# Differential attention's output norm, per tile of 128 tokens inside attention in place of per head behind it

## The chip, the cores and the metric

The kernel runs on one core of a Trainium2 chip. What counts is the device time of one execution in microseconds (us), the median of several runs. A core has five engines with a queue each that runs in order: TensorE (PE, matmuls and transposes), VectorE (DVE), ScalarE (ACT), GpSimd (POOL) and SyncE (SP), which here issues the loads. Matmul results lie in PSUM, eight banks of 512 float32 for each of 128 partitions.

## The reference, cut to what matters

A block with three token mixers, two layers deep (the delta rule "a", gated linear attention "b", differential attention "c"), whose outputs are normed, projected and merged through gates. This is the part on the third:

```python
def attend(qb, k, v):
    p = jax.nn.softmax(jnp.einsum('bhmqd,bhmkd->bhmqk', qb, k), axis=-1)
    return jnp.einsum('bhqk,bhkd->bhqd', p[:, :, 0] - lam_f * p[:, :, 1], v)
...
def out(o):
    o = _rmsnorm(o, gn) * (1.0 - lam_init)
    return o.transpose(0, 2, 1, 3).reshape(o.shape[0], o.shape[2], HC * DVC)
...
def merge(ya, yb, yd, gates):
    ga, gb, gd = jnp.split(jax.nn.sigmoid(gates), 3, axis=-1)
    return (ga * (ya @ w_o_a) + gb * (yb @ w_o_b) + gd * (yd @ w_o_c)) @ w_out
```

There are four heads of 128 output features, and 256 latent and 256 context tokens. In layer 0 all 512 tokens are queries: the first 256 (context) see 256 keys, the others 512. In layer 1 only the 256 latent tokens are queries, with 512 keys. The norm `_rmsnorm` runs over a head's 128 features, so it is independent for each token and head.

## The kernel before

Activations are kept transposed: features on the partitions, tokens along the free axis. The words of `PLAN[l]` are the steps of a layer's mixer in program order; both plans have "... hb dif mb hc ... mc": output norm of b, attention, merge of b, output norm of c, merge of c. A scheduler takes this program, and moves an instruction ahead on its engine as soon as its operands and its buffers are there, so steps that don't depend on each other interleave. Buffers come from rings: a new tile takes the next slot of its ring in program order, and can be written only when the tile that had the slot before is used up.

The rings that bear on the change: `pm`, three PSUM banks, for the chains of the stream of weight matmuls; `pq`, five PSUM banks, for everything else, attention included; `sd`, six SBUF slots with tag "d", for short-lived tiles of 512 columns, among them the square `sq` and the reciprocal root `rs` of a norm and the gates `sg` of a merge; `sm`, eight slots, for the exponentials `e` and transposed probabilities `PT` of attention.

`diff` (attention) runs over tiles of 128 queries, and in a tile over the four heads. A head is two score matmuls (L1052), for each the row maximum (L1053), its negation (L1054) and an exponential with row sums (L1056); then reciprocal, scaling and combination of both on DVE (L1059 to L1062), transposes on PE (L1065), a copy out of PSUM (L1067) and the matmuls with v (L1069, here "PV") into the bank `oc`. When four heads are done, one copy (L1070) puts the tile into `oT`, of 4 x 512 columns in layer 0, 4 x 256 in layer 1.

`head_out` for "c" goes head by head over all tokens: square (L842, ACT), a matmul with a matrix of ones that sums over the partitions (L844), into a bank of `pm`, Ln and Exp for the reciprocal root (L410 and L411, ACT), a multiply by gain and root (L853, DVE), and the split into a high and a low float32r part `yh`, `yl` (L269 ACT, L270 DVE) that the merge's matmuls read.

`merge` goes over four pairs of output chunks. For a pair it computes two gates (unless they were computed earlier and are fetched): a projection of the hidden state, PE's "pm<-hh,whl" (L274 to L276, 24 matmuls a gate), and a sigmoid of Exp, Ln and Exp on ACT (L402 to L404) in a tile `sg`. Then two chains of 12 matmuls with `wo`, "pm<-yh,whl". All stream matmuls come in threes (high by high, high by low, low by high: L274, L275, L276). L350 are the small matmuls of the modulation vectors.

Of the kernel before, what the change touches and what calls it, by code (L numbers as in the profile page):

```python
# [13 lines left out]
AF = mybir.ActivationFunctionType  # L14
OP = mybir.AluOpType
# [183 lines left out]
class Prog:  # L199
# [611 lines left out]
    def gates_ahead(self, l, j, H, count):  # L811
# [5 lines left out]
        for _ in range(count):  # L817
            pr = len(done)
            done.append(pr)
            for c, p in enumerate(self.proj(l, U_G + 3 * pr + j, H, 256 * l)):  # L820
                s = self.sd([512], "sg")[:, :n]
                self.sigmoid(s, p)
                self.nc.scalar.dma_start(g[pr // 2][:, 2 * (pr % 2) + c], s)

    def head_out(self, l, oT, gn, H, u, name):

        nc = self.nc
        c0 = 256 * l
        n = 512 - c0
        zs = self.stashed.get((l, "z" + name))  # L830
        if l == 0:
            yh = self.ch([4, 512], "yh", F32R)
            yl = self.ch([4, 512], "yl", F32R)
        else:
            y = self.ch([2, 4, 256], "yhl", F32R)
            yh, yl = y[:, 0], y[:, 1]
        for h in range(4):
            o = oT[:, h]
            if zs is None and u is not None and h % 2 == 0:
                pz = self.proj(l, u + h // 2, H, c0)  # L840
            sq = self.sd([512], "sq")
            nc.scalar.activation(sq[:, :n], o, AF.Square)  # L842
            ps = self.pm()
            nc.tensor.matmul(ps[:, :n], self.ones, sq[:, :n], start=True, stop=True)  # L844
            if zs is not None:
                rs = self.rstd(ps[:, :n], n, 1.0 / 128)
                if h == 0:
                    z = self.fetch(zs)
                nc.vector.tensor_mul(o, o, rs[:, :n])
                nc.vector.tensor_mul(o, o, z[:, h])  # L850
            elif u is None:
                rs = self.rstd(ps[:, :n], n, 1.0 / 128)
                nc.vector.scalar_tensor_tensor(o, o, gn, rs[:, :n], op0=OP.mult, op1=OP.mult)  # L853
            else:

                pv = next(pz)
                z = self.sd([512], "z")
                nc.scalar.activation(z[:, :n], pv, AF.Exp, scale=-1.0)
                nc.vector.scalar_tensor_tensor(o, o, gn, pv, op0=OP.mult, op1=OP.mult)
                nc.scalar.activation(z[:, :n], z[:, :n], AF.Ln, bias=self.one)  # L860
                nc.scalar.activation(sq[:, :n], ps[:, :n], AF.Ln, bias=self.eps, scale=1.0 / 128)
                nc.vector.scalar_tensor_tensor(z[:, :n], sq[:, :n], 0.5, z[:, :n], op0=OP.mult, op1=OP.add)
                nc.scalar.activation(z[:, :n], z[:, :n], AF.Exp, scale=-1.0)
                nc.vector.tensor_mul(o, o, z[:, :n])
            self.split(yh[:, h], yl[:, h], o)
        if self.dbg is not None and f"{name}{l}" in self.dbg:
            nc.sync.dma_start(self.dbg[f"{name}{l}"][:, :, c0:512], oT)
        return yh, yl
# [170 lines left out]
    def diff(self, l, q, k, vC):  # L1039
        nc = self.nc  # L1040
        mm = nc.tensor.matmul
        oT = self.ch([4, 512 - 256 * l], "oTc")
        for qt in range(2 * l, 4):
            nk = 256 if qt < 2 else 512
            cs = slice((qt - 2 * l) * 128, (qt - 2 * l + 1) * 128)
            o = self.pq((4, 128), "oc")
            for h in range(4):
                E, r = [], self.ti([4], "r")
                for m in range(2):
                    ms = slice(64 * m, 64 * m + 64)  # L1050
                    p = self.pq()
                    mm(p[:, :nk], q[ms, h, cs], k[ms, h, :nk], start=True, stop=True)  # L1052
                    nc.vector.tensor_reduce(r[:, m:m + 1], p[:, :nk], axis=AX.X, op=OP.max)  # L1053
                    nc.vector.tensor_scalar(r[:, m:m + 1], r[:, m:m + 1], -1.0, None, op0=OP.mult)  # L1054
                    e = self.sm([512], "e")
                    nc.scalar.activation(e[:, :nk], p[:, :nk], AF.Exp, bias=r[:, m:m + 1],  # L1056
                                         accum_out=r[:, 2 + m:3 + m])
                    E.append(e[:, :nk])
                nc.vector.reciprocal(r[:, 2:4], r[:, 2:4])  # L1059
                nc.vector.tensor_mul(r[:, 3:4], r[:, 3:4], self.nlam[l])  # L1060
                nc.vector.tensor_scalar(E[0], E[0], r[:, 2:3], None, op0=OP.mult)
                nc.vector.scalar_tensor_tensor(E[0], E[1], r[:, 3:4], E[0], op0=OP.mult, op1=OP.add)  # L1062
                tp = self.pq((4, 128), "tp")
                for j in range(nk // 128):
                    nc.tensor.transpose(tp[:, j], E[0][:, j * 128:(j + 1) * 128], self.C("ident"))  # L1065
                PT = self.sm([4, 128], "PT")
                nc.scalar.copy(PT[:, :nk // 128], tp[:, :nk // 128])  # L1067
                for j in range(nk // 128):
                    mm(o[:, h], vC[:, j, h * 128:(h + 1) * 128], PT[:, j], start=j == 0, stop=j == nk // 128 - 1)  # L1069
            nc.scalar.copy(oT[:, :, cs], o)  # L1070
        return oT


# [499 lines left out]
```

## Time and profile before

| | us |
|---|---|
| median of three runs | 2596.59 |
| lowest and highest of them | 2590.91, 2604.6 |
| the profiled execution's own time | 2588.37 |
| its span, first to last instruction | 2586.3 |
| PE busy in the span | 2444.9 (95%) |
| DVE busy | 1716.4 (66%) |
| ACT busy | 1416.6 (55%) |
| mean granted clock of PE, 1.00 being 2.4 GHz | 0.973 |

The times of instructions come from the profiled execution, so a sum of them is to be held against its 2588.37. The granted clock is 1.00 or 0.50 at any moment (2.4 or 1.2 GHz); values between are means over a stretch. Attention ("dif") of layer 0 lies at about 600 to 704 us of the span, that of layer 1 at about 1600 to 1686.

### The profile page before, as it was taken

The numbers are of one execution on the slowest core, as the hardware profiler recorded it, in microseconds if no ns is written. First come the engines' busy times: TensorE is split into PE (matmuls) and PEld (weight loads), VectorE is DVE, ScalarE is ACT, GpSimd is POOL, SyncE is SP. The second block draws the span as 40 slices with busy tenths as digits, with TensorE's granted clock in tenths as the row PEclk, the third lists the DMA queues.
The fourth block names the chain that finished last, engine by engine and source line by source line (L and its number), as shares of the span: only waits on it lengthen the run. The fifth ranks groups of instructions, "written<-read, shape, count | busy, mean of one in ns | idle before, by whom it ended". The sixth has DMA issues, their size and how long they took to land.

```text
span 2586.3 us, 35865 instructions
## 1 busy us (share of the span) xinstructions
PE 2444.9 (95%) x13712; PEld 1965.9 (76%) x13712; DVE 1716.4 (66%) x3130; ACT 1416.6 (55%) x2352; POOL 88.2 (3%) x216
## 2 busy tenths in 40 slices
PE   6998999999998999998978999998999999999997
PEld 4786776676676888886867878797878878878876
DVE  5585447756545434336684475767989888988987
ACT  4764343235553332335853433666877777777775
POOL 0000001100120000000000010010000000000000
PEclk8999899999998999999988999998999999999999
DMA  6344332122131223222362232257979899899994
GB/s 266 129 160 157 107 139 99 49 74 74 67 137 66 100 82 120 93 79 85 112 225 77 68 113 81 104 188 288 377 273 355 341 342 356 344 350 353 341 367 182
DMA packets 72707, 473.13 MB, mean 183 GB/s; under 512 B 8208, under 2 KB 10384, under 8 KB 19664
## 3 DMA queue, kind: packets, MB, share of 16 engines
q1 hardware_dynamic: 68208, 464.73, 48.3%
q10 hardware_dynamic: 4320, 6.03, 0.6%
q8 instruction: 110, 1.80, 0.3%
q14 instruction: 69, 0.57, 0.1%
HBM read 463.65 MB, written 7.08 MB: 182 GB/s over the span
## 4 chain that ended last, share of the span: by engine, by line
PE 70%; DVE 6%; ACT 3%; DMA 2%; issue 1%; POOL 0%; ACTq 0%; DVEq 0%; POOLq 0%
PE pm L275 16%; PE pm L274 16%; PE pm L276 16%; PE y L276 3%; PE y L275 3%; PE y L274 3%; PE la L985 1%; DMA raw<-in_win_dram 1%; PE pq L1052 1%; DVE whl L270 1%; PE pm L350 1%; PE tp L1352 1%; PE ob L996 1%; PE ob L998 1%; DVE zq L973 1%
## 5 line engine op out<-in xcount | busy, mean ns | idle before, releaser
L270 DVE TENSOR_TENSOR whl<-raw,whl 128x512 fp32r<-128x512 f32 (+2 forms) x490 | 330.7, 681 | 330.0 <-ACT whl L269 326.7
L274 PE MATMUL pm<-hh,whl 128*128 128x512 f32 (+2 forms) x1264 | 475.6, 378 | 21.3 <-ACT whl L269 7.8
L269 ACT CAST whl<-raw 128x512 fp32r<-128x512 f32 (+2 forms) x490 | 289.6, 600 | 357.1 <-PE pm L276 273.5
L276 PE MATMUL pm<-hh,whl 128*128 128x512 f32 (+2 forms) x1264 | 467.7, 371 | 7.4 <-DVE whl L270 7.4
L275 PE MATMUL pm<-hl,whl 128*128 128x512 f32 (+2 forms) x1264 | 468.3, 371 | 0.0
L270 DVE TENSOR_TENSOR wp<-rawc,wp 128x1024 fp32r<-128x1024 f32 x261 | 313.7, 1222 | 36.6 <-ACT wp L269 30.5
L274 PEld LDWEIGHTS pm<-hh,whl 128*128 128x128 f32 (+1 forms) x1264 | 243.0, 192 | 70.8 <-ACT whl L269 9.2
L269 ACT CAST wp<-rawc 128x1024 fp32r<-128x1024 f32 x261 | 268.1, 1051 | 21.0 <-PE y L276 11.4
L276 PEld LDWEIGHTS pm<-hh,whl 128*128 128x128 f32 (+1 forms) x1264 | 242.3, 192 | 48.9 <-DVE whl L270 8.4
L275 PEld LDWEIGHTS pm<-hl,whl 128*128 128x128 f32 (+1 forms) x1264 | 243.0, 192 | 43.2 <-issue 7.1
L270 DVE TENSOR_TENSOR wlo<-raw,whi 128x1024 fp32r<-128x1024 f32 x176 | 210.0, 1222 | 34.1 <-ACT whi L269 31.7
L275 PE MATMUL pm<-wlo,hg 128*128 128x512 f32 x530 | 212.1, 400 | 1.6 <-DVE wlo L270 1.4
L274 PE MATMUL pm<-whi,hg 128*128 128x512 f32 x530 | 211.2, 399 | 0.0
L276 PE MATMUL pm<-whi,hg 128*128 128x512 f32 x530 | 208.0, 392 | 0.0
L269 ACT CAST whi<-raw 128x1024 fp32r<-128x1024 f32 x176 | 178.9, 1052 | 13.2 <-PE pm L275 11.9
L275 PE MATMUL y<-wp,mt 128*128 128x512 f32 x348 | 135.4, 389 | 0.0
L276 PE MATMUL y<-wp,mt 128*128 128x512 f32 x348 | 135.3, 389 | 0.0
L275 PEld LDWEIGHTS pm<-wlo,hg 128*128 128x128 f32 x530 | 99.8, 188 | 34.6 <-DVE wlo L270 15.8
L274 PE MATMUL y<-wp,mt 128*128 128x512 f32 x348 | 120.1, 389 | 0.2 <-ACT mt L1354 0.2
L274 PEld LDWEIGHTS pm<-whi,hg 128*128 128x128 f32 x530 | 99.9, 189 | 20.8
L276 PEld LDWEIGHTS pm<-whi,hg 128*128 128x128 f32 x530 | 99.8, 188 | 20.2
L270 DVE TENSOR_TENSOR wlo<-rawc,whi 128x1024 fp32r<-128x1024 f32 x91 | 110.9, 1219 | 2.3 <-ACT whi L269 1.5
(394 smaller groups left out, 4528.9 us busy)
## 6 DMA issues: line engine op xcount, KB each, us to landing
rawc<-in_m_dram SPq DMA_DIRECT2D x176, 1024.0 KB, 5.4
raw<-in_m_dram SPq DMA_DIRECT2D x88, 1024.0 KB, 7.0
raw<-in_win_dram SPq DMA_DIRECT2D x64, 1024.0 KB, 5.0
raw<-in_wmod_dram SPq DMA_DIRECT2D x40, 1024.0 KB, 5.0
raw<-in_f_dram SPq DMA_DIRECT2D x22, 1024.0 KB, 4.8
raw<-in_wo_dram SPq DMA_DIRECT2D x24, 512.0 KB, 3.8
raw<-in_f_dram SPq DMA_DIRECT2D x16, 704.0 KB, 4.1
rawc<-in_wmod_dram SPq DMA_DIRECT2D x8, 1024.0 KB, 17.0
```

The lines of the kernel that those rows point to most:

```text
L269: self.nc.scalar.copy(hi, src)
L270: self.nc.vector.tensor_sub(lo, src, hi.bitcast(F32))
L274: mm(p, wh, ah, start=first, stop=False)
L275: mm(p, wh, al, start=False, stop=False)
L276: mm(p, wl, ah, start=False, stop=last)
L350: nc.tensor.matmul(p[j:j + 32, :256], self.cs[:, k, o:o + 32], w[:, k], start=i == 0 and k < 4, stop=i == n - 1 and k >= 4)
L973: nc.vector.tensor_mul(FQ[hp][r, x, a].rearrange("p (n s) -> p n s", s=LEVELS[li]), side(Fj[:, x]), side(q[hp]))
L985: mm(p[:, x % 2, hp], FK[hp][:, x], FQ[hp][:, x], start=True, stop=True)
L996: mm(o[:, hp], vB[:, tt, h * 128:(h + 1) * 128], AT[:, hp, a], start=True, stop=first)
L998: mm(o[:, hp], S[d][r, hp], qe[hp][r], start=False, stop=True)
L1052: mm(p[:, :nk], q[ms, h, cs], k[ms, h, :nk], start=True, stop=True)
L1352: nc.tensor.transpose(tp[:, a], s[:, a * 128:(a + 1) * 128], self.C("ident"))
```

## The change

A new helper `head_tile` does the norm of one tile of 128 tokens for all four heads at once: one square of 128x512, one sum into a bank of `pq`, Ln, Exp and one multiply in place. `diff` calls it behind each tile's copy, and `head_out` for "c" keeps only the split. Layer 0 has four sums of 128x512 before and after; layer 1 has two of 128x512 where it had four of 128x256. The squares and roots come from the ring "d" as before, but are taken within attention, ahead of merge b's gates in program order.

```diff
--- before.py
+++ after.py
@@ -822,6 +822,16 @@
                 self.sigmoid(s, p)
                 self.nc.scalar.dma_start(g[pr // 2][:, 2 * (pr % 2) + c], s)
 
+    def head_tile(self, o, gn):
+
+        nc = self.nc
+        sq = self.sd([4, 128], "sq")
+        nc.scalar.activation(sq, o, AF.Square)
+        ps = self.pq((4, 128))
+        nc.tensor.matmul(ps, self.ones, sq, start=True, stop=True)
+        rs = self.rstd(ps.rearrange("p a b -> p (a b)"), 512, 1.0 / 128).rearrange("p (a b) -> p a b", a=4)
+        nc.vector.scalar_tensor_tensor(o, o, gn, rs, op0=OP.mult, op1=OP.mult)
+
     def head_out(self, l, oT, gn, H, u, name):
 
         nc = self.nc
@@ -836,6 +846,9 @@
             yh, yl = y[:, 0], y[:, 1]
         for h in range(4):
             o = oT[:, h]
+            if name == "c":
+                self.split(yh[:, h], yl[:, h], o)
+                continue
             if zs is None and u is not None and h % 2 == 0:
                 pz = self.proj(l, u + h // 2, H, c0)
             sq = self.sd([512], "sq")
@@ -1068,6 +1081,7 @@
                 for j in range(nk // 128):
                     mm(o[:, h], vC[:, j, h * 128:(h + 1) * 128], PT[:, j], start=j == 0, stop=j == nk // 128 - 1)
             nc.scalar.copy(oT[:, :, cs], o)
+            self.head_tile(oT[:, :, cs], self.A["gnc", l])
         return oT
```

Behind the first hunk the line numbers grow: scores are L1065 after (L1052 before), transposes L1078 (L1065), PV L1082 (L1069), the exponentials L1069 (L1056). The square is L829 and the sum L831.

PE's queue in the middle of layer 0's attention, in the heads with 512 keys, before ("x4" joins four equal instructions in a row):

```order
L274 MATMUL pm<-yh,whl 128x512
L1065 MATMUL tp<-cstt,e 128x128 x4
L1052 MATMUL pq<-kC,qC 128x512 x2
L1069 MATMUL oc<-PT,vC 128x128 x4
L275 MATMUL pm<-yl,whl 128x512
L276 MATMUL pm<-yh,whl 128x512
L274 MATMUL pm<-yh,whl 128x512
L275 MATMUL pm<-yl,whl 128x512
L276 MATMUL pm<-yh,whl 128x512
L274 MATMUL pm<-yh,whl 128x512
```

The same engine and place after, around the third tile's sum:

```order
L1078 MATMUL tp<-cstt,e 128x128 x4
L1065 MATMUL pq<-kC,qC 128x512
L1082 MATMUL oc<-PT,vC 128x128 x4
L1065 MATMUL pq<-kC,qC 128x512
L1078 MATMUL tp<-cstt,e 128x128 x4
L1082 MATMUL oc<-PT,vC 128x128 x4
L831 MATMUL pq<-sq,ones 128x512
L1065 MATMUL pq<-kC,qC 128x512 x2
L1078 MATMUL tp<-cstt,e 128x128 x4
L1082 MATMUL oc<-PT,vC 128x128 x4
```

No stream matmul stands between these heads any more. PE's queue at the last tile's sum of layer 0, after:

```order
L1078 MATMUL tp<-cstt,e 128x128 x4
L1082 MATMUL oc<-PT,vC 128x128 x4
L831 MATMUL pq<-sq,ones 128x512
L274 MATMUL pm<-yh,whl 128x512
L275 MATMUL pm<-yl,whl 128x512
L276 MATMUL pm<-yh,whl 128x512
```

The stream matmuls of merge b that stood between heads have moved behind this sum: 168 up to merge c in layer 0 (24 for two chains, 48 for two gates, and so on), and 240 of 128x256 in layer 1.

ACT's queue behind the first tile of layer 0's attention, before:

```order
L1067 COPY PT<-tp 128x256
L1070 COPY oTc<-oc 128x4x128
L1056 ACTIVATE e,r<-pq,r 128x256 x2
L402 ACTIVATE sg<-pm 128x512
L1067 COPY PT<-tp 128x256
L403 ACTIVATE sg<-sg,cb 128x512
L269 CAST whl<-raw 128x512
L404 ACTIVATE sg<-sg 128x512
L1056 ACTIVATE e,r<-pq,r 128x256 x2
```

The first of the gates that follow, after, which stands at the last tile's end:

```order
L1069 ACTIVATE e,r<-pq,r 128x512 x2
L1080 COPY PT<-tp 128x512
L1083 COPY oTc<-oc 128x4x128
L829 ACTIVATE sq<-oTc 128x512
L410 ACTIVATE rs<-pq,cb 128x512
L402 ACTIVATE sg<-pm 128x512
L411 ACTIVATE rs<-rs,cb 128x512
L403 ACTIVATE sg<-sg,cb 128x512
```

Merge b's gate (L402) stood one tile into attention before, and stands behind the last tile's `rs` after. On DVE each tile's multiply stands between the first row maximum of the next tile and its negation. On SP the two residual loads of layer 0 stand ahead of six weight loads which they followed before. POOL's order is the same.

## Rows read from the trace of the kernel before

**Rows 1.** The page: busy time of the engines; chain that ended last, by engine.

```profile
PE 2444.9 (95%) x13712; PEld 1965.9 (76%) x13712; DVE 1716.4 (66%) x3130; ACT 1416.6 (55%) x2352; POOL 88.2 (3%) x216
...
PE 70%; DVE 6%; ACT 3%; DMA 2%; issue 1%; POOL 0%; ACTq 0%; DVEq 0%; POOLq 0%
```

**Rows 2.** Windows: length, busy PE PEld DVE ACT POOL (instructions), PEclk, DMA share, GB/s.

```profile
648.11:701.48 53.37, 50.80 (x229) 34.24 (x230) 29.70 (x69) 26.92 (x59) 3.37 (x2) 1.00 0.15 54
722.00:771.00 49.00, 49.00 (x218) 40.55 (x218) 21.70 (x31) 25.04 (x43) 11.55 (x7) 1.00 0.33 115
1705.68:1714.57 8.89, 8.87 (x74) 8.70 (x73) 6.88 (x12) 7.25 (x17) 2.12 (x2) 1.00 0.74 258
```

**Rows 3.** Timeline (start, us, what), PE, attention of layer 0, then 1.

```profile
641.96 0.71 PE L1069 MATMUL oc<-PT,vC 128*128 128x128 f32 x4
...
1640.78 0.66 PE L1065 MATMUL tp<-cstt,e 128*128 128x128 f32 x4
...
1643.50 1.12 PE L1052 MATMUL pq<-kC,qC 64*128 64x512 f32 x2
```

**Rows 4.** Chain of waits (start, us, what) in one head, layer 1.

```profile
1665.23 1.11 PE pq L1052 x4
1666.34 0.68 DVE r L1053
...
1667.05 0.16 DVE r L1054
...
1668.02 0.79 ACT e L1056 x2
...
1669.19 0.40 DVE e L1061
...
1669.66 0.45 issue
1670.11 0.76 DVE e L1062
...
1670.91 0.66 PE tp L1065 x4
```

**Rows 5.** Timeline, last tile's end in layer 0 and the first sum.

```profile
701.13 0.39 PE L274 MATMUL pm<-yh,whl 128*128 128x512 f32 x1
701.48 0.66 PE L1065 MATMUL tp<-cstt,e 128*128 128x128 f32 x4
...
704.01 0.59 ACT L1070 COPY oTc<-oc 128x512 f32<-128x512 f32 x1 [1.25 <-PE oc L1069]
...
705.43 1.06 PE L844 MATMUL pm<-sq,ones 128*128 128x512 f32 x2
...
706.43 1.07 PE L350 MATMUL pm<-raw,cs 128*32 128x256 f32 x16
...
708.44 0.75 DVE L853 SCALAR_TENSOR_TENSOR oTc<-oTc,gnc,rs 128x512 f32<-128x512 f32 x1 [1.47 <-ACT rs L411]
```

**Rows 6.** Timeline, the last sum and merge c's start in both layers.

```profile
713.88 2.07 PE L844 MATMUL pm<-sq,ones 128*128 128x512 f32 x2 [1.30 <-ACT sq L842]
...
714.97 1.42 PE L274 MATMUL pm<-yh,whl 128*128 128x512 f32 x1
...
721.89 0.50 PE L274 MATMUL pm<-hh,whl 128*128 128x512 f32 x1
...
1689.31 0.33 SPq L250 DMA_DIRECT2D raw<-in_wo_dram  x1
...
1694.37 0.58 PE L274 MATMUL pm<-yhl,whl 128*128 128x256 f32 x1 [1.77 <-ACT whl L269]
```

**Rows 7.** PE after a long wait: timeline, then windows as in rows 2.

```profile
212.07 0.79 PE L274 MATMUL pm<-hh,whl 128*128 128x512 f32 x1 [4.44 <-DVE zs L807]
...
212.00:214.00 2.00, 1.93 (x5) 1.55 (x6) 0.73 (x3) 1.33 (x2) 1.24 (x1) 0.50 0.34 131
215.00:217.00 2.00, 2.00 (x17) 0.94 (x19) 0.76 (x2) 1.96 (x3) 0.00 (x0) 0.91 0.00 0
```

## The prediction

> **What bounds the kernel now.** I read the page's engine totals and its chain shares first. TensorE (PE) is busy 95% of the span and holds 70% of the chain that ended last; DVE and ACT hold 6% and 3% [rows 1]. So work on DVE or ACT costs nothing as long as PE has matmuls ready to run beside it, and the question for any edit is whether PE's queue stays filled. Then I read two stretches by windows. Over seven of the eight 512-key heads of layer 0's attention (648.11 to 701.48) PE is busy 50.80 of 53.37 us at full clock, which is a head in 53.37 / 7 = 7.62 us [rows 2]. The timelines show why: merge b's matmuls (L274 to L276) run right up to a head's transposes (L1065), and score and PV matmuls (L1052, L1069) are short pieces among them [rows 3, 5]. Those stream matmuls alone run at 49.00 / 218 = 0.225 us each (128x512, layer 0) and 8.89 / 74 = 0.120 us (128x256, layer 1) [rows 2].
>
> Last, the chain of waits in a head of layer 1 shows what a head costs by itself, without that cover: scores 1.11, row maximum, negation, two exponentials, two scalings, combination, then transposes. From the scores' end (1666.34) to the transposes' start (1670.91) are 4.57 us, of which 0.45 is an issue gap on DVE [rows 4]. I take 4.12 us for the bare softmax. In these 4.12 us PE has nothing of attention to do.
>
> **What is removed.** Behind attention, the sums of `head_out` for "c" run as a chain in layer 0: the first sum (L844) starts at 705.43, the fourth at 713.88, and merge c's first chain starts at 714.97 at half clock [rows 5, 6]. It goes: −9.5 us at most if merge c could start right behind merge b, less the L350 block of 1.07 us that runs there anyway [rows 5]. In layer 1 merge c's start at 1694.37 waits for weights whose load was issued at 1689.31 [rows 6], so little is won there (2 us at most). ACT and DVE do the same four normalizations in layer 0 and the same bytes in two in place of four in layer 1, which only saves overhead on engines that don't bind.
>
> **What is added.** At each tile's end stand a square, a sum of 128x512, Ln, Exp and a multiply. Sum and multiply have rows, 1.06 and 0.75 [rows 5]. Beside a filled PE the norm would cost the sum's 1.06 us alone, which is only moved; the rest would hide behind stream matmuls.
>
> **What is moved, and this decides.** The square and the `rs` of a tile come from the six-slot ring "d" in SBUF. Merge b's gate tiles `sg` come from the same ring, and stand later in the program. In the changed order the first of merge b's remaining Exp of a gate (L402 `sg`) on ACT stands behind the last tile's `rs` (L410), where it stood behind tile 0 before. With it, PE's whole rest of merge b goes behind the last tile's sum (L831): 168 matmuls of 128x512 in layer 0, 240 of 128x256 in layer 1. What remains in front is bare: three 256-key heads and eight 512-key heads in layer 0, the last five heads in layer 1. PE waits there for softmax, behind the head's own score matmuls; merge b's matmuls, queued behind these in order, can't fill in, and merge c waits for them. The SP queue brings the two residual loads ahead of six weight loads in layer 0; those are needed only after attention too, so I put that at nothing, hidden by the 38 us of matmuls below. POOL's order is unchanged.
>
> A bare tile of four 512-key heads, all from rows:
> - First head: scores 1.11, softmax 4.12 [rows 4], and 0.95 for the previous tile's multiply, which stands on DVE in front of the first negation (0.75 [rows 5], and 0.2 that I allow for its release): 6.18.
> - A head whose next scores stand behind its PV: transposes to the PV's end 701.48 to 704.01 is 2.53 [rows 5], plus 1.11 and 4.12: 7.76.
> - A head whose next scores are split around its PV (two of three steps): transposes at 1640.78 to the second score's end at 1644.62 is 3.84 [rows 3]; the first maximum and one exponential (0.79, [rows 4]) are by then done, so 4.12 − 0.79 = 3.33 remain: 7.17.
> - End: transposes to copy 2.53, copy and square to the sum's start 704.01 to 705.43 is 1.42, sum 1.06 [rows 5]: 5.01.
> Sum 6.18 + 7.76 + 2 x 7.17 + 5.01 = 33.3 us.
>
> **Layer 0.** Tile 1's last PV ended at 641.96 + 0.71 = 642.67 [rows 3]. Its bare heads of 256 keys I leave at their old time (lower bound) plus 2.5 for tile 0's square and sum ahead of the next scores; with its own 1.42 + 1.06 tile 1 ends at 647.6. Two tiles of 33.3 end at 714.2. Then 168 x 0.225 = 37.8, the L350 block 1.1, and merge c's first 24 matmuls 5.4: its first gate matmul would start at 758.5, where it started at 721.89 [rows 6]. That is +36.6, and +1.5 for the block's start at half clock: +38.
>
> **Layer 1.** The second head's transposes stay at 1640.78 [rows 3]. One split head (7.17) and an end (5.01) give 1652.9, one tile 1686.2, 240 x 0.120 = 28.8 give 1715.0; L350's first unit 1.3 (1.07 [rows 5] and 0.2 to release the load), then from merge c's load to its first matmul 1694.37 − 1689.31 = 5.06 [rows 6]: 1721.4 against 1694.37, +27, with a start at half clock of 2.5 about +29.
>
> **The clock.** Bare, PE idles 3.3 to 4.1 us in every head. Before, a wait of 4.44 us was followed by a granted clock of 0.50 (the 1.2 GHz level), which rose again some 3 us later, 0.91 in the window from 215 [rows 7]. At half clock a sum takes 2.07 [rows 6] in place of 1.06 [rows 5]; I take a factor of 1.85, since a score matmul is 1.12 [rows 3]. PE's pieces on a bare tile's chain are 1.11 + 2.83 + 2 x 3.84 + 2.78 = 14.4 us; all at half clock they cost 0.85 x 14.4 = 12.2 more, for three tiles 36.7, for the rest of layer 1's first tile 5.6, for 256-key heads about 4.5: 47 in all. None at half clock is the lower bound, 0. I take three fifths, 28, because the bursts of a split head (3.84 at full clock) are long enough to see the clock rise before they end, as at 212 to 215, while scores alone are not.
>
> **The sum.** 38 + 29 + 28 = +95 on the profiled execution's 2588.4: 2683. That execution is 8.2 under the median of 2596.6, so as a median 2691.
>
> **Rivals.**
> (1) Half clock throughout: +47 in place of 28, 2711. For it: the fourth sum, after a wait of only 1.30 us, ran at half clock, 2.07 us [rows 6]. Against: the rise in 3 us. The Trainium skill ("TensorE: Matmul & The Clock Gate", section "HAM oscillation — how this bites in real kernels") says that a loop whose bursts of matmuls are shorter than the waits between them finds the array's clock lowered anew in each round; by that rule this rival holds, 2711. The rows above show single such events, and no attention without cover, so the trace doesn't settle it.
> (2) Full clock throughout: 2596.6 + 67 = 2664. It needs that score and PV matmuls keep the clock up across 4.12 us of waiting; 212.07 speaks against [rows 7].
> (3) Two heads' softmax run side by side. DVE's work in a head is two maxima of 0.68, four small operations like the negation's 0.16, 0.40 and 0.76: 3.2 us [rows 4], so a head could take half of 7.2. Over the 13 heads that the sum prices, 4.0 less each gives 52 back: 2664 − 52 = 2612, still a little slower. Against: PE's order has the next head's scores behind this head's transposes, so there is one softmax at a time.
> (4) The change does only what it says, merge b's matmuls still fill attention, and the sums' chain behind it goes: 9.5 − 1.07 − the last tile's copy and square 1.42 = 7 less in layer 0, 2 less in layer 1, so 2588, not slower. It decides as soon as merge b's gates stand ahead of the last tile's `rs` on ACT, which the order doesn't have. The Trainium skill ("Perfetto Trace Analysis", section "Matmuls") wants independent matmul groups to rotate through different PSUM banks so that one group's evacuation overlaps the next group's matmuls; the sums' move from the stream's three banks to attention's five is in its sense, and by it alone the time would be this 2588. No row speaks of banks as the wait that ends last here; the ring in SBUF decides.
>
> **How the numbers follow.** Partly half clock 0.52, rival 1 0.26, rival 2 0.15, rival 3 0.04, rival 4 0.03. The likeliest gives 2691. Only the last 7 in 100 and part of rival 2 may be left out, so the range goes from 2650, below full clock by a head or two that runs shorter, to 2716, above half clock by the spread of runs (5 to 8 us). A measurement of this kernel tells about 0.5% (13 us) from no change: faster by more has 0.01, within it 0.04, slower 0.95.
>
> **What would show it.** In the changed profile: attention's stretches with PE busy about half in place of 95%, no L274 to L276 between heads of tiles 2 and 3; 7.2 to 8.5 us a head; a granted clock well under 1 there; a block of some 38 us of merge b behind the last L831 with PE full; layer 0 about 50 us longer at merge c, layer 1 about 40. I would be wrong if heads take under 6 us, or if merge b's matmuls run between them.

## The result, and the profile after

The changed kernel takes 2699.9 us (median of 4 runs, 2695.81 to 2710.29) against 2595.44 before: a ratio of 1.0409, 95% interval 1.0379 to 1.0438, slower. It was forecast at 2691, in a range of 2650 to 2716.

The profiled execution took 2697.81 us, 109.4 more than that of before (2588.37). The page, engine totals and the granted clock in 40 slices of some 67 us, after:

```profile
PE 2491.2 (92%) x13708; PEld 1989.6 (74%) x13708; DVE 1717.3 (64%) x3128; ACT 1419.1 (53%) x2346; POOL 87.4 (3%) x216
...
PE   6998999996699899998988999688999999999997
...
PEclk8999899997599899998989999688999999999999
```

DVE and ACT are busy as long as in [rows 1], within 3 us. PE shows 46 us more busy time for four records less (layer 1 now has two sums where it had four): the same matmuls, some of them slower. The loss lies at two places, slices 10 and 11 (layer 0's attention) and 26 and 27 (layer 1's), where the clock falls to 5 to 8 tenths.

The same stretch as [rows 3] and on to merge c, PE's timeline after (start, us, what, idle before and its releaser). L1078 are the transposes, L1065 scores, L1082 PV, L831 the tile's sum:

```profile
645.38 2.08 PE L831 MATMUL pq<-sq,ones 128*128 128x512 f32 x2 [1.34 <-ACT sq L829]
647.38 2.08 PE L1065 MATMUL pq<-kC,qC 64*128 64x512 f32 x4
654.23 1.08 PE L1078 MATMUL tp<-cstt,e 128*128 128x128 f32 x4 [4.77 <-DVE e L1075]
655.99 2.08 PE L1082 MATMUL oc<-PT,vC 128*128 128x128 f32 x8 [0.68 <-ACT PT L1080]
658.00 2.08 PE L1065 MATMUL pq<-kC,qC 64*128 64x512 f32 x4
664.22 1.11 PE L1078 MATMUL tp<-cstt,e 128*128 128x128 f32 x4 [4.15 <-DVE e L1075]
665.26 2.07 PE L1065 MATMUL pq<-kC,qC 64*128 64x512 f32 x2
667.26 2.07 PE L1082 MATMUL oc<-PT,vC 128*128 128x128 f32 x8
669.27 2.07 PE L1065 MATMUL pq<-kC,qC 64*128 64x512 f32 x2
674.70 1.11 PE L1078 MATMUL tp<-cstt,e 128*128 128x128 f32 x4 [3.36 <-DVE e L1075]
...
690.50 2.08 PE L831 MATMUL pq<-sq,ones 128*128 128x512 f32 x2 [1.34 <-ACT sq L829]
...
735.63 2.08 PE L831 MATMUL pq<-sq,ones 128*128 128x512 f32 x2 [1.34 <-ACT sq L829]
...
738.98 0.80 PE L274 MATMUL pm<-yh,whl 128*128 128x512 f32 x1 [1.26 <-ACT sg L402]
...
742.98 0.63 PE L274 MATMUL pm<-yh,whl 128*128 128x512 f32 x1
743.41 0.60 PE L275 MATMUL pm<-yl,whl 128*128 128x512 f32 x1
743.84 0.41 PE L276 MATMUL pm<-yh,whl 128*128 128x512 f32 x1
```

No stream matmul stands between the heads. PE waits 4.77, 4.15 and 3.36 us for softmax (released by L1075, the combination on DVE), and each score, sum and PV takes 2.07 or 2.08. Before, the scores took 1.12 [rows 3], the sum 1.06 [rows 5] and the eight PV matmuls of a head 1.16:

```profile
1642.41 1.16 PE L1069 MATMUL oc<-PT,vC 128*128 128x128 f32 x8
```

A tile is 690.50 − 645.38 = 45.1 us. The first stream matmul behind the last sum is released by `sg` (L402), a gate's sigmoid: the bank it needs was held by a finished gate projection that ACT could not read out before.

The windows of one bare tile in each layer and of merge b's block behind the last sum (columns as in rows 2):

```profile
690.50:735.63 45.13, 26.70 (x66) 13.49 (x66) 13.08 (x34) 11.31 (x25) 0.00 (x0) 0.50 0.08 25
739.00:779.50 40.50, 40.50 (x168) 33.08 (x168) 17.70 (x23) 20.21 (x35) 8.49 (x5) 0.94 0.22 78
1718.83:1763.97 45.14, 26.70 (x67) 13.50 (x67) 13.27 (x34) 11.34 (x25) 0.00 (x0) 0.54 0.00 1
```

Against [rows 2] PE is busy 59% of a tile in place of 95%, and its matmuls run at 1.2 GHz throughout (the 0.54 of layer 1's tile is taken up in the last section); the block of 168 matmuls then fills PE wholly.

Where the time came from is read at two steps that both kernels share, merge c's first gate projection in layer 0 and its first matmul in layer 1, after:

```profile
786.18 0.39 PE L274 MATMUL pm<-hh,whl 128*128 128x512 f32 x1
...
1803.43 0.58 PE L274 MATMUL pm<-yhl,whl 128*128 128x256 f32 x1 [3.60 <-ACT whl L269]
```

The first was at 721.89 [rows 6], so it is 64.3 us later; the second was at 1694.37 and is 109.1 later, so layer 1 adds 44.8. Nothing before or behind adds to it: the whole profiled execution is 109.4 longer.

### The profile page after: what moved, and what is told of

Read it like the earlier page. It is cut to its first block, busy times and chain, and to the rows that moved or that the text cites. A ratio compares the mean times of both kernels' runs of the same rounds, so it can differ in the third digit from the quotient of the medians.

```text
span 2695.7 us, 35871 instructions
## 1 busy us (share of the span) xinstructions
PE 2491.2 (92%) x13708; PEld 1989.6 (74%) x13708; DVE 1717.3 (64%) x3128; ACT 1419.1 (53%) x2346; POOL 87.4 (3%) x216
## 4 chain that ended last, share of the span: by engine, by line
PE 72%; DVE 6%; ACT 4%; issue 1%; DMA 1%; ACTq 0%; DVEq 0%
PE pm L275 17%; PE pm L274 17%; PE pm L276 16%; PE y L276 3%; PE y L275 3%; PE y L274 3%; PE pq L1065 2%; PE oc L1082 1%; PE la L998 1%; ACT e L1069 1%; PE pm L350 1%; PE tp L1078 1%; PE tp L1366 1%; PE ob L1009 1%; PE ob L1011 1%
```

## The experiments

Theory R: the ring of SBUF slots "d" puts merge b's gates behind the last tile's norm, with them PE's stream, and bare attention runs slow, first for want of cover (stream matmuls that fill PE's waits) and second at half clock. Rival N: the norm itself, tile by tile on the path of softmax, is the price. Rival B: the sums take one of attention's five banks. Ratios are to the kernel before, run on the same chip (medians 2591 to 2594 us).

**The norm without the ring of gates.** The changed kernel, square and root from the ring of exponentials:

```diff
-        sq = self.sd([4, 128], "sq")
+        sq = self.sm([4, 128], "sq")
...
-        rs = self.rstd(ps.rearrange("p a b -> p (a b)"), 512, 1.0 / 128).rearrange("p (a b) -> p a b", a=4)
+        rs = self.sm([4, 128], "rs")
+        nc.scalar.activation(rs, ps, AF.Ln, bias=self.eps, scale=1.0 / 128)
+        nc.scalar.activation(rs, rs, AF.Exp, bias=self.zero, scale=-0.5)
```

> The changed kernel with one difference: the square and the root of head_tile take slots of the eight-slot ring of attention's exponentials in place of the six-slot ring of the gates. The norm's work, its place and its bank are the same. Theory R (the ring puts merge b's gates, and with them its matmuls, behind the last tile): in the built order 9 to 42 stream matmuls stand between heads again, so the 67 us of lost cover and the 37 to 42 us of half clock both go, and the sums' chain behind attention stays away: 2588 us, between 2580 and 2597. Rival N (the norm of each tile on the path of the softmax is what costs: six squares, sums and multiplies) and rival B (the sums take one of attention's five banks): as the changed kernel, 2690 to 2705.

Measured: 2596.49 us, ratio 1.0015 (1.0004 to 1.0026). The loss of 104 us is gone with nothing else changed in the norm's work or banks; B falls, and N as an explanation of it. But it is some 4 us slower than before, not 4 faster: something of N is left. The window of a tile from sum to sum, and the end of layer 0's attention on PE, in this kernel (here L1080 are the transposes):

```profile
643.14:676.02 32.88, 31.06 (x145) 21.04 (x144) 19.00 (x41) 17.91 (x36) 3.37 (x2) 1.00 0.14 53
```

```profile
700.75 0.66 PE L1080 MATMUL tp<-cstt,e 128*128 128x128 f32 x4 [0.55 <-DVE e L1077]
...
707.97 0.66 PE L1080 MATMUL tp<-cstt,e 128*128 128x128 f32 x4 [2.37 <-DVE e L1077]
...
712.71 2.08 PE L831 MATMUL pq<-sq,ones 128*128 128x512 f32 x2 [1.34 <-ACT sq L829]
```

The clock is at 1.00 and PE at 94% in the tile. The last head, though, is bare (a wait of 2.37): attention ended 8 us later than before, counted from the first sum of b's norm (575.80 here, 577.26 before: 132.2 us to the last transposes, against 124.2), so merge b ran out first. From the last transposes to merge c it took 9.8 us against 13.5. The last experiments take this up.

**The ring without the norm.** The kernel before, with two tiles of the ring taken behind each query tile and one column of each written:

```diff
             nc.scalar.copy(oT[:, :, cs], o)
+            for name in ("sq", "rs"):
+                nc.scalar.copy(self.sd([4, 128], name)[:, :, 0], oT[:, :, cs.start])
```

> The kernel before with one addition: behind each tile's copy, two tiles of the ring of gates are taken and a single column of each is written by two small copies on ACT (128x4). No norm, no sum and no bank is moved; the norm stays behind merge b. Theory R: the gates wait for the last tile as in the changed kernel, no stream matmul stands between the bare heads (the built order has 168 and 240 behind them), so 2685 us, between 2670 and 2700: the changed kernel less the wait for square and sum at each tile's end (about 2 to 4 us for six tiles, partly at half clock). Rivals N and B: neither norm nor bank has moved, so 2595 us, as the kernel before.

Measured: 2689.84 us, ratio 1.0384 (1.0364 to 1.0403). Twelve copies of 128x4 cost 97 us, by the slots that they write to. With e1 this settles the cause: the ring alone brings the loss, the norm without the ring does not.

**One slot, once.** The same with a single tile of the ring behind the last query tile of each layer (`for name in ("rs",) if qt == 3 else ()`):

> The kernel before with one addition: behind the last tile's copy of each layer a single tile of the ring of gates is taken and one column of it is written (128x4, ACT). One of six slots is taken, once. If what blocks the gates is that the ring hands out its slots in program order (a gate's tile, later in the program, can't be taken before this one, which waits for the last tile), the cover is lost as in e2: the built order has 168 and 240 matmuls behind the last heads and none between the bare ones; 2690 us, 2680 to 2697. If it is the number of slots that runs out (eight of the norm's tiles against six slots), one slot more or less costs little: 2592 to 2600.

Measured: 2694.86 us, ratio 1.0395 (1.0359 to 1.0430). Five of the six slots stay for gates, and the loss is the same. So the ring does not run out; it hands out its slots in program order. PE in the middle of layer 0's attention of this kernel (lines of before: transposes L1065, scores L1052, PV L1069), no norm anywhere near:

```profile
678.27 1.11 PE L1065 MATMUL tp<-cstt,e 128*128 128x128 f32 x4 [3.42 <-DVE e L1062]
679.32 2.07 PE L1052 MATMUL pq<-kC,qC 64*128 64x512 f32 x2
681.32 2.08 PE L1069 MATMUL oc<-PT,vC 128*128 128x128 f32 x8
683.32 2.07 PE L1052 MATMUL pq<-kC,qC 64*128 64x512 f32 x2
688.81 1.11 PE L1065 MATMUL tp<-cstt,e 128*128 128x128 f32 x4 [3.42 <-DVE e L1062]
```

The head has the same 10.5 us, the same waits and durations as in the changed kernel.

**Two slots at the first tile only** (`("sq", "rs") if qt == 2 * l else ()`):

> As e2, with the two tiles taken behind the first tile of each layer only. In layer 0 the first gates follow at once, as before the change: no loss there. In layer 1 the first tile ends in the middle of attention, and the built order has two nearly bare heads in front of it (2 and 0 stream matmuls between transposes in place of 32 and 28) and 48 of 128x256 more behind the last head: 48 x 0.12 = 6 us, and 2 to 7 us of half clock: 2600 to 2606, that is 8 to 13 above the kernel before. If any use of the ring within attention cost the whole cover: 2690.

Measured: 2607.24 us, ratio 1.0058 (1.0036 to 1.0079): 14 us, a little over the 8 to 13 expected. In layer 0 merge c's first gate starts at 721.78, as before (721.89 [rows 6]); in layer 1 merge c starts at 1710.45 in place of 1694.37. The loss goes by where in attention the slot is taken.

**The clock apart from the cover.** The changed kernel with ten dummy matmuls in each bare head of 512 keys:

```diff
+                if qt >= 2 and not (l == 1 and qt == 2 and h < 3):
+                    for j in range(10):
+                        mm(o[:, h], self.C("ident"), self.C("ident"), start=True, stop=True)
                 nc.vector.reciprocal(r[:, 2:4], r[:, 2:4])
```

> The changed kernel with dummy work on PE: in each bare 512-key head (eight in layer 0, five in layer 1) ten matmuls of 128x128 float32 behind the scores, into the head's own slice of the output bank, which the real matmuls overwrite. They are to keep PE busy while softmax runs, nothing waits for their result. A matmul of this kind is 1.16 / 4 = 0.29 us at full clock by the PV rows, so ten are 2.9 us in a wait of 3.4 to 4.8 us. If the half clock is what a bare tile costs beyond 33 us (45.1 measured): tiles of about 34 to 36 us, the three tiles and the rest of layer 1's first save 30 to 40 us, 2660 to 2670. If the clock stays at half in spite of them, ten take 5.4 us, more than the wait, and the time rises above 2700, by some 20 us. If the long durations of scores and PV in the changed kernel are not the clock but something of the head itself: 2700, no change.

Measured: 2672.83 us, ratio 1.0309 (1.0292 to 1.0326), that is 27 us less than the changed kernel by more work, a little short of the 30 to 40 expected. Its three bare tiles, and a head's pieces on PE (L1074 are the dummies, L1081 transposes, L1085 PV):

```profile
653.80:688.20 34.40, 27.94 (x146) 18.36 (x146) 13.14 (x33) 11.19 (x24) 0.00 (x0) 0.92 0.00 0
688.20:723.04 34.84, 28.52 (x146) 19.66 (x146) 13.17 (x34) 11.30 (x25) 0.00 (x0) 0.87 0.11 35
1709.87:1743.53 33.66, 27.33 (x144) 19.24 (x145) 13.36 (x34) 11.33 (x25) 0.00 (x0) 0.87 0.00 1
```

```profile
662.66 0.63 PE L1081 MATMUL tp<-cstt,e 128*128 128x128 f32 x4 [1.53 <-DVE e L1078]
663.22 1.12 PE L1065 MATMUL pq<-kC,qC 64*128 64x512 f32 x2
664.27 1.16 PE L1085 MATMUL oc<-PT,vC 128*128 128x128 f32 x8
665.36 1.12 PE L1065 MATMUL pq<-kC,qC 64*128 64x512 f32 x2
666.41 2.50 PE L1074 MATMUL oc<-cstt 128*128 128x128 f32 x20
669.84 0.66 PE L1081 MATMUL tp<-cstt,e 128*128 128x128 f32 x4 [0.93 <-DVE e L1078]
```

Scores are back at 1.12 and PV at 1.16, and a split head (the next scores stand around its PV) is 669.84 − 662.66 = 7.18 us, where it was 10.5. The tiles are 33.7 to 34.8 in place of 45.1. So the long durations are the clock, and it costs 10 to 11 us a tile. What is left is 80 us, 2672.8 against 2592.5. I put it down to the cover (67 in the prediction's sum), to the half clock that the dummies left, and to the 256-key heads and each attention's last sum, which have no dummies; no run separates these.

**The sums in the stream's banks.** `self.pm((4, 128))` in place of `self.pq((4, 128))` in `head_tile`:

> The changed kernel with the sums of head_tile in the stream's three banks, as before the change, in place of attention's five. Rival B (a bank of attention's five is what is missing): 2700 or less. Theory R extended to any ring that both share: the stream's chains now wait for each tile's sum too. In the built order no stream matmul stands between the second head and the last sum in either layer: against the changed kernel 72 matmuls of 128x512 (72 x 0.225 = 16 us) and 48 of 128x256 (48 x 0.12 = 6 us) of cover more are lost, and more heads run at half clock: 2722 to 2735.

Measured: 2709.36 us, ratio 1.0456 (1.0438 to 1.0473). The sign is as R has it: a shared ring of banks blocks as a ring of slots does. The size was wrong, 9 to 12 us (by medians or by ratios) and not 22 to 35. I had put the 72 and 48 matmuls that moved behind as a loss in full. In layer 0 the 72 (16 us) cost nearly that: from the last sum's start to the L350 block behind merge b are 57.0 us (730.70 to 787.74), against 43.9 in the changed kernel (735.63 to 779.56), 13 more. But the last sum comes 5 us earlier, because here the next tile's scores stand on PE ahead of the sum:

```profile
648.07 2.07 PE L1065 MATMUL pq<-kC,qC 64*128 64x512 f32 x2
650.07 2.07 PE L831 MATMUL pm<-sq,ones 128*128 128x512 f32 x2
653.50 1.11 PE L1078 MATMUL tp<-cstt,e 128*128 128x128 f32 x4 [1.35 <-DVE e L1075]
...
694.80 1.11 PE L1078 MATMUL tp<-cstt,e 128*128 128x128 f32 x4 [1.36 <-DVE e L1075]
```

Behind the sum PE waits 1.35 us for softmax in place of 4.77, and from this tile's first transposes to the next tile's are 41.3 us (653.50 to 694.80) in place of 45.1 (654.23 to 699.36). So merge b ends 8 us later in layer 0, not 16.

**The bank alone.** The kernel before, `ps = self.pq() if name == "c" else self.pm()` in `head_out`:

> The kernel before with one part of the change alone: the four sums of head_out for c take banks of attention's five in place of the stream's three; their place behind attention, head by head, stays. The second and fourth sum waited for their squares on ACT, not for a bank, so theory R expects no change: ratio 0.998 to 1.002. If the rule on rotating banks were what is worth something here, the chain of sums from 705 to 715 would shrink by the waits of 0.35, 2.48 and 1.30 us, about 4 us in layer 0 and 1 in layer 1: ratio 0.998 at most, likely 0.9975 to 0.998.

Measured: 2591.63 us, ratio 0.9995 (0.9981 to 1.0008). The part of the change that concerns banks is worth nothing that can be measured.

**The norm one head later.** From e1, the norm of a tile is written behind the next tile's first head:

```diff
+        todo = []
...
+                if h == 0 and todo:
+                    self.head_tile(todo.pop(), self.A["gnc", l])
             nc.scalar.copy(oT[:, :, cs], o)
-            self.head_tile(oT[:, :, cs], self.A["gnc", l])
+            todo = [oT[:, :, cs]]
+        self.head_tile(todo.pop(), self.A["gnc", l])
```

> The kernel of the ring of exponentials (e1) with the norm of a tile written one head later: behind the next tile's first head, the last tile's at the end. In e1 a tile took 32.9 us where it took 28 to 29 before; theory R2: there the next tile's scores stood on PE behind the sum, which waited for copy and square, and DVE had the multiply in front of a negation, so the path of softmax grew by the norm's length, 8 us up to the last transposes in layer 0, of which the shorter tail (9.8 in place of 13.5 us from the last transposes to merge c) gave 3.7 back. One head later the sum stands behind scores that are already under way: tiles of 29 to 30 us, last transposes 2 to 4 us later than before, the same short tail: 0 to 4 us faster than before per kernel, 2588 to 2593, ratio 0.998 to 1.000. Rival: it is the norm's work itself (more PE, ACT and DVE work within attention) that stretches the tiles, wherever it stands: as e1, ratio 1.001 to 1.003.

Measured: 2587.31 us, ratio 0.9988 (0.9975 to 1.0002), against 1.0015 (1.0004 to 1.0026) of e1. PE at the last tile's end in this kernel (L1081 transposes):

```profile
650.62 1.02 PE L831 MATMUL pq<-sq,ones 128*128 128x512 f32 x2
...
682.75 1.02 PE L831 MATMUL pq<-sq,ones 128*128 128x512 f32 x2
...
703.15 0.66 PE L1081 MATMUL tp<-cstt,e 128*128 128x128 f32 x4 [0.49 <-DVE e L1078]
...
706.98 1.12 PE L831 MATMUL pq<-sq,ones 128*128 128x512 f32 x2
```

No sum waits for its square in these rows any more, not the last either, which runs at full clock (1.12 against 2.08 in e1). The last transposes come 126.6 us behind b's first sum (576.53), 2.4 later than before, where e1 was 8 later. So most of e1's stretch came from where the norm stands, not from its work. The tile shown is still 32.1 us from sum to sum (29 to 30 expected, 32.9 in e1): the gain lies mostly in the other tiles. This kernel and the next are the fastest here, but the interval still holds no gain.

**And without the last copy**, the last tile's square and multiply reading the output bank:

> As e6, with the last tile's copy out of the bank left out: its square and its multiply read the output bank, and the multiply writes the output. The copy is 0.59 us on the tail of each layer. Where the tail sets merge c's start, 1.2 us less than e6 in all (ratio lower by 0.0005); in layer 1, where merge c's start also waits for its weights' load, possibly none: then 0.6 us, within the noise.

Measured: 2586.69 us, ratio 0.9984 (0.9969 to 1.0000): the copy's share is inside the noise, as expected. Against before it is 4 us at best; the two intervals of e6 and e7 end at 1.0002 and 1.0000, so a gain is likely but not shown.

## Why the prediction was right, point by point

- **What decides** was the ring's order, not the norm. Right: e1 takes the ring away and the loss goes, e2 and e8 use the ring alone and the loss comes. The prediction read it from the built order, with `sg` behind the last `rs`; e8 adds that a single slot suffices.
- **The bare tile**: 33.3 us from the rows, 45.5 with all of PE's pieces at half clock. Measured 45.1 after, and 33.7 to 34.8 with the dummies, at 0.87 to 0.92 of the clock. The parts fit too: a split head 7.17 forecast, 7.18 measured in e3.
- **Layer 0**: tile 1 was to end at 647.6; its sum ended at 645.38 + 2.08 = 647.5. That it agrees so closely is partly luck: the forecast was for full clock, and the last pieces ran at half. At merge c +38 was forecast at full clock, +64.3 came: 26 more, 24 of them in the two bare tiles (45.1 for 33.3). **Layer 1**: +29 forecast, +44.8 came: 16 from the clock. (The head at 1640.78, called the second in the prediction, is the tile's third; the sum counts from there rightly.)
- **The clock** is the term that was mis-sized. I took three fifths of 47 us, 28; 42 came (109.4 less the 67 of the sum at full clock), nine tenths; PE's busy time grew by 46 us. A head took 10.0 to 10.5 us, not the 7.2 to 8.5 that I named as a sign. The step that failed: that a split head's burst is long enough for the clock to rise within it, as at 212 to 215 [rows 7]. At half clock the burst at 664.22 is 1.11 and three times 2.07 us without a gap, 7 us, and its last piece is as slow as its first. Rival 1 was right for nearly all of it: granted clock 0.50 and 0.54 over whole tiles. The Trainium skill ("TensorE: Matmul & The Clock Gate", section "HAM oscillation — how this bites in real kernels") describes a loop whose bursts of matmuls are shorter than the waits between them, with the clock lowered anew in each round. The trace agrees in the outcome but not in the condition: the split heads' bursts, 7 us at half clock, are longer than the waits of 3.4 to 4.8 us between them. Three fifths came from a single event of stream matmuls, not from a row of bare attention.
- **The total**: on the profiled execution's base 2683 forecast, 2697.8 measured, by those 14 us. On the medians 2691 against 2699.9. Rival 1's 47 us would have given 2702 on the profiled base, nearer than the forecast: the time lies in the range, but the case that I held likeliest is not the one that came.
- **Rival 4** (only the sums' chain goes, 2588) is what e1 was to give. It gave 2596.5: the 9 us for the chain were right in direction (tail 13.5 to 9.8 us in layer 0), but I had costed the norm within attention as hidden by stream matmuls. In e1 the next tile's scores stand behind the sum on PE and wait with it for copy and square; cover hides PE's idling, not the lengthening of the chain of softmax. With the norm one head later (e6) the time is 2587.3, which bears this out.
- **The rule on banks** (the Trainium skill, "Perfetto Trace Analysis", section "Matmuls") has nothing to act on here, as the prediction had it: e5 shows no change, and e4 shows that the stream's banks would be the worse place, by some 10 us.

## What to carry to other kernels

Where buffers come from a ring in program order, one early use that waits for a late event holds up every later user of that ring, even with slots free, and whatever hangs on those users on other engines. Before moving a step, ask which ring its temporaries come from, and who takes the next slot. Work that is small beside its neighbours can cost through what it displaces: here moving six short norms cost 109 us, by the prediction's sum 67 for lost cover and the other 42 for the clock that fell when PE had only a dependent chain to run.

## What the runs showed of the hardware

- In layer 0's bare tiles PE, busy 59%, held 1.2 GHz for all of 45 us, through bursts of 7 us without a gap. Merge b's stream at the same level rose 4.9 us after its start (738.98 to 743.84, where its rows go from 0.63 to 0.41 us; its block of 40.5 us has a mean of 0.94). Ten dummy matmuls of 128x128 in each wait brought 0.87 to 0.92, and 27 us of the whole.
- In layer 1's bare tile the clock did rise once, and no matmul ran in it. These are the windows of a burst of PV and scores, of the wait behind it, and of the next head's burst, after:

```profile
1729.45:1733.54 4.09, 4.09 (x12) 2.29 (x12) 0.00 (x0) 0.00 (x0) 0.00 (x0) 0.50 0.02 4
1734.00:1737.00 3.00, 0.00 (x0) 0.00 (x0) 2.02 (x8) 1.56 (x4) 0.00 (x0) 1.00 0.00 0
1738.00:1744.00 6.00, 6.00 (x16) 3.17 (x14) 0.85 (x2) 1.36 (x3) 0.00 (x0) 0.50 0.00 0
```

So PV and scores can be followed by a rise, and the dummies of e3, of PV's own shape, were too: the sum before them took 2.08 us (653.80), the transposes behind them 0.63 (662.66). Why the longer bursts of the split heads did not raise the clock is open; no run here took them apart.
- Two score matmuls of 64 rows issued together took 1.11 us as one did alone [rows 3, 4] (2.08 for both at half clock, 2.07 for one): they run side by side.
